# Hybrid short-convolution and SSD step: pools, early loads and the order of splits where the projection hands over to the mixing

## The chip, the cores and the metric

The kernel runs on one core of a Trainium2 chip. The core has TensorE (PE in the profile, with its weight loads as PEld), VectorE (DVE), ScalarE (ACT), GpSimd (POOL) and SyncE (SP, which here issues all DMAs), each with an instruction stream of its own, in order; semaphores tie the streams together. The metric is the time of one execution in device microseconds, the median of several runs.

## The reference

One layer over 2048 prompt tokens and 64 sample tokens, width 1024, all float32. Cut to what matters:

```python
h = rmsnorm(x, norm_in_w) * (1 + scale) + shift        # shift, scale, gate = split(c @ w_mod + b_mod)
proj = h @ w_in                                         # (1024, 7184): the large product
b_gate, c_gate, h_a, g_a, z, xbc_raw, dt_raw = split(proj)
y_a = rmsnorm(b_gate * dwconv3(c_gate * h_a) * silu(g_a), norm_a_w)
xs, bs, cs = split(silu(dwconv4(xbc_raw) + conv_b_b))
y = ssd(xs, softplus(dt_raw + dt_bias), -exp(a_log), bs, cs) + d_skip * xs   # causal scan in chunks
y_b = rmsnorm(y * silu(z), norm_b_w)
x = x + gate * (concat(y_a, y_b) @ w_out)               # (2048, 1024): the output product
y_out = rmsnorm(x, norm_f_w)
```

`c` has one row for the prompt and one for the sample. The states of both convolutions and of the scan are outputs too.

## The kernel before, in words

Every large product is made of three: each operand is split into a high part (rounded by ACT's copy) and a low part (the rest, by DVE), and high x high, high x low and low x high are added up in PSUM. The weights of the output product are split the same way by `split_wo(k, raw)`: ACT writes the high part `woh` (line 1274), DVE the low part `wol` (line 1275), from a raw row block of 512 KB that SP has loaded (`wo_raw`). There are 16 such blocks.

**Projection (`phase_project`).** The tokens go through in two passes. A pass visits 28 pairs of feature tiles (`work[g]`, 56 in all): z, x/B/C and the four parts of the convolution branch. The features and tokens of a pair are cut in quarters so that seven products (`s` = 0 to 6) do the work of eight; sums and differences of quarters (A22, A12, A11, S1 to S4) are kept in SBUF. In each slot `s` the code issues a product on PE (line 282), prepares a weight quarter of the next pair (`w_hi` on ACT, line 248; `w_lo` on DVE, line 239), runs hooks, runs work from a queue with an estimated cost (`run_bg`), and empties PSUM (`evac`: copies `keep` on ACT at line 307, adds on DVE at line 315). `w_load(g + 2)` loads the raw weights of a pair, 1 MB, two pairs ahead. Everything is written in program order; no scheduler moves it.

The rows that are worked on live in tiles `row0` to `row7`. Hooks in pairs 51 to 53 compute the gate (`gate_load`, `gate_part`): eight blocks of `w_mod` are multiplied with `c`, then four adds put the bias on, tile `gb` (line 635); each bias piece is loaded just ahead of its add (line 633) and the result stored right after it (line 636).

**The last pair (`last_pair`, g = 55).** It is done as eight plain products from S1, A22, A12 and A11 in that order (line 1169), each emptied from its own two PSUM banks: `evac_last(1, ...)` after S1 and A22, `evac_last(0, ...)` after the others (lines 487 and 489, into the rows `c_row`, which are then stored to `va_d`, line 492). Its weights come from `last_w` (lines 175 and 176). While PE works, nine of the 16 output weight blocks are split, and the decays of the first chunk, tiles `lt`, are computed by `decay_first` (lines 1195 and 1197: eight Relu and one Exp each).

**Mixing (`phase_mix`).** For each chunk of 128 tokens and each half of the heads: `ssd1` (PE heads and transposes, lines 1335 to 1339; DVE then makes `bc`, `xd`, `lt`, `xe`, lines 1344 to 1351), `ssd2` (PE, lines 1363 to 1369), `join1` and `join2` on DVE; and for each token tile the output product with both branches, `out_mm` (lines 1438 and 1445; `vah` is the split convolution branch, `vbh` the split SSD branch). `ra` is the inverse norm of a branch (`inv_rms`: PE, DVE, POOL). It starts with the 64 sample tokens, mixed with the first chunk; there the other seven weight blocks are split. `vb_s` is the sample's SSD branch, loaded from `vb_d` and split by ACT and DVE (lines 1411 and 1415).

Pools are stacked from both sides of SBUF. A tile of a later pool waits for the readers of the tiles it overlies; a tile with the same tag waits for the readers of the one before it.

Of the kernel before, what the change touches and what calls it, by code (L numbers as in the profile page):

```python
# [27 lines left out]
def kernel(  # L28
# [76 lines left out]
    def phase_project():  # L105
# [14 lines left out]
        lp = pool(stack, "lp", bufs=1, reuse_waits="tile")  # L120
        hs1 = pool(hstack, "hs1", bufs=1, side="right", reuse_waits="tile")
# [60 lines left out]
        for i in (0, 1, 6, 7, 2, 3, 4, 5):  # L182
            row(i, [128, 1094], f"row{i}_")
        pad(lp, "pad_l", 128)
        raws = [hs1.tile([128, KT, 256], F32, tag=f"raw{i}", name=f"raw{i}") for i in range(2)]
        pad(hs1, "pad_h", 96)
# [317 lines left out]
        def dt_parts():  # L504
# [6 lines left out]
            def load():  # L511
# [386 lines left out]

        sample = sample_parts()
# [19 lines left out]
        def mod_half(half, pieces):  # L919
# [11 lines left out]
            m = stats.tile([128, 2, 4, 2], F32, tag="mcol", name="mcol", bufs=1)  # L931
# [225 lines left out]

        def last_pair():
# [3 lines left out]
            pss = {fh: [bank(no + u) for u in range(2)] for fh, no in (((0, 1), 4), ((1, 1), 2), ((0, 0), 0), ((1, 0), 6))}  # L1162
# [10 lines left out]
            p1 = mix["sp1"] = pool(ctx, "sp1", side="right", reuse_waits="tile")  # L1173
            state = mix["state"] = p1.tile([128, 2, 512], F32, tag="state", name="state")
            fast = [p1.tile([128, 8, 128], F32, tag="lt", name="lt", bufs=2) for _ in range(2)]
            p1.tile([128, 8, 128], F32, tag="rb", name="rb_")
            xbs = [p1.tile([128, 8, 128], F32, tag="xb", name="xb", bufs=2) for _ in range(2)]
            pad(p1, "pad_p", 224)
# [11 lines left out]
            def load_decay(hf):  # L1190
                SP.dma_start(out=fast[hf], in_=r_d[hf * 8:hf * 8 + 8, :].partition_broadcast(128))

            def decay_first(hf):
                for h in range(8):
                    ACT.activation(out=fast[hf][:, h, :], in_=fast[hf][:, h, :], func=AF.Relu, scale=-1.0,
                                   bias=acum[:, 0, 8 * hf + h:8 * hf + h + 1])
                ACT.activation(out=fast[hf], in_=fast[hf], func=AF.Exp, scale=-1.0)
                held[0, hf] = fast[hf]

            va = mix["va"] = state[:, 1, :].rearrange("p (s t) -> p s t", t=NS_TOK)  # L1200
# [476 lines left out]
```

## Time and profile before

| what | value |
|---|---|
| median of 3 runs | 1759.02 us (1757.54 to 1760.46) |
| the profiled execution, whole | 1758.51 us |
| its span, first to last instruction | 1756.7 us |
| TensorE's mean granted clock | 0.994 of full |
| DVE busy | 74% of the span |
| ACT busy | 47% |
| DMA, mean over the span | 125 GB/s |
| HBM read, written | 164.31 MB, 54.15 MB |

The span is what the profiler saw of the instructions; the time is taken around the whole execution and is 1.8 us longer. "A <- B" in the waits reads: A stood idle until B had finished. Rows of a timeline give the start, the duration, the engine, the line, output <- inputs, and in brackets the idle time ahead and what ended it. Times in them count from the start of the span.

### The profile page before, as it was taken

The page shows a single profiled execution, that of the slowest core. Times are in us where ns is not written, and L with a number is a line of the kernel's source. Part 1 is how long each engine was busy: PE and PEld are TensorE (multiplying, and loading weights), DVE is VectorE, ACT ScalarE, POOL GpSimd, SP SyncE. Part 2 cuts the span into 40 slices and gives each one's busy share as a digit, 9 for nine tenths or more (in the row PEclk, how much of TensorE's full clock was granted, in tenths as well). Part 3 has the DMA queues.
Part 4 walks back from the last instruction along what each step waited for, and adds up shares of the span by engine and source line. Part 5 has one row for each costly group of instructions (what it writes and reads, how often), then busy time and mean ns, then how long its engine had stood idle before and what let it go on. Part 6 is the DMA issues. An engine that isn't in the chain of part 4 may idle for free.

```text
span 1756.7 us, 27034 instructions
## 1 busy us (share of the span) xinstructions
PE 1713.1 (98%) x10585; PEld 1511.0 (86%) x10585; DVE 1307.6 (74%) x2026; ACT 828.4 (47%) x1579; POOL 102.9 (6%) x224
## 2 busy tenths in 40 slices
PE   5999999999999999999999999999899999999998
PEld 4788888887888899999999999989588888888887
DVE  5787779776677746687768767646788888888885
ACT  5644344444653645334333444325455555545552
POOL 0000000000000000010001000000011111101011
PEclk9999999999999999999999999999899999999999
DMA  9223323233538832312322242424653343434341
GB/s 340 73 73 96 96 82 99 84 104 102 168 127 296 294 100 80 97 54 95 100 75 74 74 121 79 131 73 161 200 192 125 139 150 126 161 107 169 110 150 36
DMA packets 186867, 220.21 MB, mean 125 GB/s; under 512 B 21316, under 2 KB 152372, under 8 KB 186740
## 3 DMA queue, kind: packets, MB, share of 16 engines
q1 hardware_dynamic: 186740, 218.49, 37.7%
q8 instruction: 83, 1.36, 0.3%
q14 instruction: 44, 0.36, 0.1%
HBM read 164.31 MB, written 54.15 MB: 124 GB/s over the span
## 4 chain that ended last, share of the span: by engine, by line
PE 89%; DVE 3%; ACT 3%; DMA 2%; issue 2%; SPq 0%; POOL 0%; POOLq 0%; ACTq 0%; DVEq 0%
PE bank L282 58%; PE mm L1438 14%; PE mm L1445 7%; PE sd L1363 2%; PE sd L1367 2%; PE sd L1369 2%; DMA praw<-in_w_mod_dram 1%; PE sd L1335 1%; PE sd L1339 1%; PE bank L1048 1%; PE bank L535 0%; PE bank L536 0%; DVE loS L1035 0%; PE bank L826 0%; PE sd L1337 0%
## 5 line engine op out<-in xcount | busy, mean ns | idle before, releaser
L282 PE MATMUL bank<-hiS,w 128*128 128x272 f32 (+1 forms) x2560 | 596.6, 322 | 5.7 <-ACT keep L307 5.6
L282 PEld LDWEIGHTS bank<-hiS,w 128*128 128x128 f32 x2560 | 431.0, 189 | 41.5 <-ACT keep L307 8.2
L282 PE MATMUL bank<-hiA,w 128*128 128x272 f32 (+1 forms) x1920 | 447.8, 321 | 3.1 <-DVE z_row L315 2.7
L282 PE MATMUL bank<-loS,w 128*128 128x272 f32 (+1 forms) x1280 | 411.4, 321 | 0.0
L282 PEld LDWEIGHTS bank<-hiA,w 128*128 128x128 f32 x1920 | 322.8, 188 | 30.8 <-DVE z_row L315 3.2
L239 DVE TENSOR_TENSOR w<-raw,w 128x512 fp32r<-128x512 f32 x318 | 217.7, 687 | 161.7 <-ACT w L248 150.8
L248 ACT CAST w<-raw 128x512 fp32r<-128x512 f32 x318 | 196.3, 622 | 240.2 <-PE bank L282 134.3
L282 PE MATMUL bank<-loA,w 128*128 128x272 f32 (+1 forms) x960 | 308.1, 321 | 0.0
L282 PEld LDWEIGHTS bank<-loS,w 128*128 128x128 f32 x1280 | 241.4, 189 | 16.1
L282 PEld LDWEIGHTS bank<-loA,w 128*128 128x128 f32 x960 | 180.5, 188 | 12.2
L307 ACT COPY keep<-bank 128x272 f32<-128x272 f32 (+1 forms) x240 | 106.0, 451 | 133.4 <-PE bank L282 132.8
L388 DVE SCALAR_TENSOR_TENSOR acc<-raw_row,par,acc 128x1024 f32<-128x1024 f32 (+1 forms) x96 | 126.4, 1317 | 2.0
L239 DVE TENSOR_TENSOR raw<-raw 128x512 f32<-128x512 f32 x161 | 111.0, 689 | 3.7
L1438 PE MATMUL mm<-woh,vah 128*128 128x512 f32 (+1 forms) x272 | 109.5, 403 | 0.0
L1438 PE MATMUL mm<-wol,vah 128*128 128x512 f32 (+1 forms) x272 | 106.5, 392 | 0.0
L1438 PE MATMUL mm<-woh,vbh 128*128 128x512 f32 (+1 forms) x256 | 103.7, 405 | 0.0
L1438 PE MATMUL mm<-wol,vbh 128*128 128x512 f32 (+1 forms) x256 | 100.5, 392 | 0.0
L1297 ACT ACTIVATE lt<-rb,acum 128x128 f32<-128x128 f32 x240 | 73.3, 388 | 3.7 <-DMA rb<-r_d 3.2
L248 ACT CAST w<-t 128x512 fp32r<-128x512 f32 x53 | 32.8, 618 | 76.2 <-PE bank L282 76.2
L1445 PE MATMUL mm<-woh,vah 128*128 128x512 f32 (+1 forms) x272 | 67.3, 390 | 0.0
L1445 PE MATMUL mm<-woh,vbh 128*128 128x512 f32 (+1 forms) x256 | 63.3, 389 | 0.0
L1445 PEld LDWEIGHTS mm<-woh,vah 128*128 128x128 f32 (+1 forms) x272 | 50.2, 185 | 11.5
(298 smaller groups left out, 2375.2 us busy)
## 6 DMA issues: line engine op xcount, KB each, us to landing
raw<-in_w_in_dram SPq DMA_DIRECT2D x56, 1024.0 KB
xb_d<-acc SPq DMA_DIRECT2D x32, 512.0 KB
xb<-xb_d SPq DMA_DIRECT2D x32, 512.0 KB
rb<-r_d SPq DMA_DIRECT2D x30, 512.0 KB
xt<-in_x_prompt_dram SPq DMA_DIRECT2D x16, 512.0 KB
praw<-in_w_mod_dram SPq DMA_DIRECT2D x16, 512.0 KB
z_d<-z_row SPq DMA_DIRECT2D x16, 512.0 KB
va_d<-c_row SPq DMA_DIRECT2D x16, 512.0 KB
```

The source lines that it names most:

```text
L239: DVE.tensor_tensor(out=out, in0=a, in1=b, op=ALU.subtract)
L248: ACT.copy(out=w[:, 0], in_=w_src(g, j))
L282: PE.matmul(ps[:, 0:n], w[:, a, k, :], h[:, k, o:o + n], start=(s in (0, 1, 5) and k == 0 and i == 0), stop=(k == 3 and i == 2), skip_grou ...
L307: ACT.copy(out=keep[s][:, o:o + n], in_=b["y" if s == 1 else "x"][:, 0:n])
L388: DVE.scalar_tensor_tensor(out=acc[:, 0:n], in0=r[:, k:k + n], scalar=cb_w(k, t), in1=acc[:, 0:n], op0=ALU.mult, op1=ALU.add)
L1048: PE.matmul(ps, w[:, a, k, :], x, start=(i == 0 and k == 0 and n == 0), stop=(i == 1 and k == 3 and n == 2))
L1297: ACT.activation(out=lt[:, h, :], in_=rb[:, h, :], func=AF.Relu, scale=-1.0, bias=acum[:, c, h0 + h:h0 + h + 1])
L1363: PE.matmul(py4[64 * e:64 * e + 64, j, :], xd[:, 2 * j + e, :], lt[:, 2 * j + e, :], start=True, stop=True)
L1367: PE.matmul(po4[:, j, :], state[:, hf, j * 128:(j + 1) * 128], xb[:, 6 + j // 2, :], start=True, stop=True)
L1369: PE.matmul(ps[:, g * 256:(g + 1) * 256], bc[:, g, :], xe[:, 4 * g:4 * g + 4, :].rearrange("p h q -> p (h q)"), start=True, stop=True)
L1438: PE.matmul(ps[:n], hl[:, 0, k, 0:n], wo[k0 + k][i][:, nn * 512:(nn + 1) * 512], start=(k == 0 and i == 0), stop=False)
L1445: PE.matmul(ps[:n], hl[:, 1, k, 0:n], wo[k0 + k][0][:, nn * 512:(nn + 1) * 512], start=False, stop=(k == 7))
```

## The change

Three things are changed, all around the end of the projection.

1. *Pools.* Rows 2 to 5 and the raw weights go into a pool `top` that stays open to the end, where the last pair and the mixing use the same tiles again (`row4` for `rb` and weight blocks, `row5` for `state`, `raw0` and `raw1` for `xb` and `lt`, rows 2 and 3 for output weight 6). The pool `sp1` goes. The raw weights of a pair become two tiles of 512 KB with a DMA each. Some small tiles move from `stats` to `lp`. In PSUM the last pair takes its banks in another order, and the mixing phase opens its tag `mm` first.
2. *Loads.* The four bias pieces of the gate are loaded with the gate's first block. In pair 54 SP loads the first half of chunk 0 (`load_first(0)`) and the first four output weight blocks (`early_o`), and ACT computes the first decay in slot 4 of that pair. In the mixing phase three weight blocks are loaded ahead of `vb_s`.
3. *Splits.* Eleven blocks are split in the last pair (0 to 10), 11 to 13 ahead of the sample's `ra`, and 14 and 15 after the first half of chunk 0. In a slot, `last_w` comes after `evac`.

```diff
         def row(i, shape, name, dtype=F32):
             flush(i)
-            return (hs1 if 2 <= i <= 5 else lp).tile(shape, dtype, tag=f"row{i}", name=name)
+            return (top if 2 <= i <= 5 else lp).tile(shape, dtype, tag=f"row{i}", name=name)
...
-            raw = raws[g % 2] = hs1.tile([128, KT, 256], F32, tag=f"raw{g % 2}", name="raw")
+            raw = raw_pair()
             col = work[g][0]
-            SP.dma_start(out=raw, in_=w_in[:, col:col + 256].rearrange("(k p) f -> p k f", p=128))
+            for i in range(2):
+                SP.dma_start(out=raw[i], in_=w_in[512 * i:512 * i + 512, col:col + 256].rearrange("(k p) f -> p k f", p=128))
...
         def gate_load(k, r):
+            if k == 0:
+                gb = gate_held["gb"] = row(4, [128, 256], "gb")
+                for j in range(4):
+                    SP.dma_start(out=gb[32 * j:32 * j + 2, 0:256], in_=b_mod[:, 2 * D + j * 256:2 * D + (j + 1) * 256]
+                                 .partition_broadcast(2).rearrange("p o n -> p (o n)"))
...
-                gb = row(4, [128, 256], "gb")
+                gb = gate_held["gb"]
                 for j in range(4):
                     q, col = slice(32 * j, 32 * j + 2), slice(j * 256, (j + 1) * 256)
-                    SP.dma_start(out=gb[q, 0:256], in_=b_mod[:, 2 * D + j * 256:2 * D + (j + 1) * 256]
-                                 .partition_broadcast(2).rearrange("p o n -> p (o n)"))
                     DVE.tensor_tensor(out=gb[q, 0:256], in0=ps[q, 0:256], in1=gb[q, 0:256], op=ALU.add)
                     SP.dma_start(out=g_d[:, col], in_=gb[q, 0:256])
...
+        hook_at(54 * 7, lambda: load_first(0))
+        for k in range(4):
+            hook_at(54 * 7 + 1 + k // 2, lambda k=k: early_o(k))
...
+        def load_first(hf):
+            fast[hf] = top.tile([128, 8, 128], F32, tag="raw1", name="lt", bufs=2)
+            SP.dma_start(out=fast[hf], in_=r_d[hf * 8:hf * 8 + 8, :].partition_broadcast(128))
+            xbs[hf] = top.tile([128, 8, 128], F32, tag="raw0", name="xb", bufs=2)
+            SP.dma_start(out=xbs[hf], in_=xb_d[0, :, hf])
+            loads[0, hf] = [xbs[hf], None]
...
+        def early_o(k):
+            raw_o[k] = row(2 + k, [128, D], "wo_raw")
+            SP.dma_start(out=raw_o[k], in_=w_out[k * 128:(k + 1) * 128, :])
...
-            pss = {fh: [bank(no + u) for u in range(2)] for fh, no in (((0, 1), 4), ((1, 1), 2), ((0, 0), 0), ((1, 0), 6))}
+            pss = {fh: [bank(no) for no in nos] for fh, nos in (((0, 1), (4, 5)), ((1, 1), (6, 7)), ((0, 0), (3, 2)), ((1, 0), (0, 1)))}
...
-            homes = ["w6", "rb", "row6", "row7", "w6", "rb", "row6", "row7", "w6"]
+            homes = [None] * 4 + ["w6", "row7", "row6", "row4", "w6", "row7", "row6", "row4"]
...
-            for k in range(9):
+            load_o(4)
+            load_o(5)
+            load_first(1)
+            load_o(6)
+            for k in range(11):
                 split_wo(k, raw_o.pop(k))
-                if k + 4 < 9:
+                if k == 2:
+                    load_o(7)
+                elif k == 3:
...
+                elif 4 <= k <= 7:
                     load_o(k + 4)
-                if k < 2:
-                    decay_first(k)
-                elif k == 5:
+                if k == 5:
+                    decay_first(1)
                     evac_last(1, True)
                     evac_last(1, False)
-            evac_last(0, False)
+                elif k == 9:
+                    evac_last(0, False)
...
-                elif s > 0:
+                evac(p, g, s)
+                if tg >= last and s > 0:
                     last_w(s - 1)
-                evac(p, g, s)
+                if (g, s) == (last - 1, 4):
+                    decay_first(0)
...
+        for k, tag, bufs in ((12, "xr", 2), (13, "xr", 2), (14, "gate", 1)):
+            load_o(k, tag, bufs)
         vb = sp.tile([128, 8, 128], F32, tag="vb", name="vb_s")
         SP.dma_start(out=vb[:, :, 0:n], in_=vb_d)
         for hf in range(2):
             prefetch_z(0, hf)
...
+        load_o(15, "nf", 1)
...
         va = prefetch_va(0)
+        for k in (11, 12, 13):
+            split_wo(k, raw_o[k])
         ra = inv_rms(sqa, n, "ra")
         t0 = take_a(16, pa, ra)
-        for k, nxt, tag, bufs in ((9, 13, "xr", 2), (10, 14, "xr", 2), (11, 15, "gate", 1), (12, None, "", 0)):
-            split_wo(k, raw_o[k])
...
-            split_wo(k, raw_o[k])
-            if nxt:
-                load_o(nxt, tag, bufs)
...
-        for k in (13, 14, 15):
+        for k in (14, 15):
             split_wo(k, raw_o[k])
```

How the instructions stand, before and after, at three places. Line numbers of the changed kernel are its own.

SP's queue from the gate's last two bias pieces (`gb` the bias tile, `g_d` the gate in DRAM) into the last pair, before:

```order
L633 DMA gb<-in_b_mod_dram 2x256
L636 DMA g_d<-gb 2x256
L1188 DMA wo_raw<-in_w_out_dram 128x1024
L1191 DMA lt<-r_d 128x1024
L1188 DMA wo_raw<-in_w_out_dram 128x1024
L1191 DMA lt<-r_d 128x1024
L1188 DMA wo_raw<-in_w_out_dram 128x1024 x2
L1215 DMA xb<-xb_d 128x1024 x2
```

and after, from the four stores of the gate:

```order
L654 DMA g_d<-gb 2x256 x4
L1183 DMA lt<-r_d 128x1024
L1185 DMA xb<-xb_d 128x1024
L1197 DMA wo_raw<-in_w_out_dram 128x1024 x4
L1222 DMA wo_raw<-in_w_out_dram 128x1024 x2
L1183 DMA lt<-r_d 128x1024
L1185 DMA xb<-xb_d 128x1024
```

The bias loads no longer stand between the stores, and the first decay's rows, the first `xb` and four weight blocks are issued in the pair before the last.

ACT from the fourth weight of the last pair (line 175, in the changed kernel 178) to the first output weight blocks (`woh`), before:

```order
L175 CAST w_11394<-raw 128x512
L462 ACTIVATE g_row<-g_row 128x1090
L175 CAST w_11429<-raw 128x512
L175 CAST w_11459<-raw 128x512
```

and, a few rows on,

```order
L462 ACTIVATE g_row<-g_row 128x1090
L1274 ACTIVATE woh_11683<-wo_raw,par 128x1024
L1195 ACTIVATE lt<-lt,acum 128x128 x8
L1197 ACT_TABLE_LOAD
L1197 ACTIVATE lt<-lt 128x1024
L1274 ACTIVATE woh_11685<-wo_raw,par 128x1024
L1195 ACTIVATE lt<-lt,acum 128x128 x8
L1197 ACTIVATE lt<-lt 128x1024
```

After, from the same weight:

```order
L178 CAST w_11535<-raw 128x512
L1190 ACTIVATE lt<-lt,acum 128x128 x8
L1192 ACT_TABLE_LOAD
L1192 ACTIVATE lt<-lt 128x1024
L477 ACT_TABLE_LOAD
L477 ACTIVATE g_row<-g_row 128x1090
L178 CAST w_11578<-raw 128x512
```

The first decay stands ahead of the Silu of `g_row` and of the last two weights, with a table load on either side of it.

DVE from the split of the sample's SSD branch to the first chunk's second half, before:

```order
L1415 TENSOR_TENSOR vbh<-vb_s,vbh 128x8x64
L100 TENSOR_SCALAR ms<-sd 64x1
L1275 SCALAR_TENSOR_TENSOR wol_11700<-wo_raw,par,woh_11699 128x1024
L1275 SCALAR_TENSOR_TENSOR wol_11702<-wo_raw,par,woh_11701 128x1024
L1275 SCALAR_TENSOR_TENSOR wol_11704<-wo_raw,par,woh_11703 128x1024
L1275 SCALAR_TENSOR_TENSOR wol_11706<-wo_raw,par,woh_11705 128x1024
L1378 SCALAR_TENSOR_TENSOR yt<-xb,dcol,sd 128x128 x4
L1344 TENSOR_TENSOR bc<-sd,cst 128x256
L1346 TENSOR_TENSOR xd<-sd,dt_t 128x512
L1349 TENSOR_TENSOR lt<-lt,bc 128x512 x2
```

and after:

```order
L1444 TENSOR_TENSOR vbh<-vb_s,vbh 128x8x64
L1302 SCALAR_TENSOR_TENSOR wol_11841<-wo_raw,par,woh_11840 128x1024
L1302 SCALAR_TENSOR_TENSOR wol_11843<-wo_raw,par,woh_11842 128x1024
L1302 SCALAR_TENSOR_TENSOR wol_11845<-wo_raw,par,woh_11844 128x1024
L102 TENSOR_SCALAR ms<-sd 64x1
L1407 SCALAR_TENSOR_TENSOR yt<-xb,dcol,sd 128x128 x4
L1373 TENSOR_TENSOR bc<-sd,cst 128x256
L1375 TENSOR_TENSOR xd<-sd,dt_t 128x512
L1378 TENSOR_TENSOR lt<-lt,bc 128x512 x2
```

Three splits instead of four, and they stand ahead of `ms`, the DVE step of `ra`, where four stood behind it.

More of the change, by code (lines that the diff above doesn't have):

```diff
@@ L81, in pad @@
         p.tile([128, n // 4], F32, tag=name, name=name, bufs=1)
+    pad(const, "pad_c", 64)
     def ca_w(k, t):
@@ L181, in phase_project, with raw_pair @@
             h_tile(q, 544)
[L182 to L186, printed above, removed]
+        for i in (0, 1, 6, 7, 2, 3, 5, 4):
+            row(i, [128, 1152 if i in (2, 3) else 1094], f"row{i}_")
+        for _ in range(2):
+            lp.tile([128, 4, 2], F32, tag="ss", name="ss", bufs=2)
+            lp.tile([128, 4], F32, tag="ms4", name="ms4", bufs=2)
+        lp.tile([128, 2, 4, 2], F32, tag="mcol", name="mcol")
+        lp.tile([128, NH], F32, tag="dtb", name="dtb")
+        lp.tile([128, NH], F32, tag="alog", name="alog")
+        pad(lp, "pad_l", 64)
+        pad(top, "pad_t", 192)
+        def raw_pair():
+            return [top.tile([128, 4, 256], F32, tag=f"raw{i}", name="raw", bufs=2) for i in range(2)]
+        for _ in range(2):
+            raw_pair()
+        pad(top, "pad_e", 224)
         def load_rows(chunks, rows):
@@ L1156, in last_w, with decay_first @@
             split(src, w[:, 0], w[:, 1])
+        raw_o, fast, xbs = {}, {}, {}
+        def load_first(hf):
[4 more added lines that the diff above has]
+            loads[0, hf] = [xbs[hf], None]
+        def decay_first(hf):
+            for h in range(8):
+                ACT.activation(out=fast[hf][:, h, :], in_=fast[hf][:, h, :], func=AF.Relu, scale=-1.0,
+                               bias=acum[:, 0, 8 * hf + h:8 * hf + h + 1])
+            ACT.activation(out=fast[hf], in_=fast[hf], func=AF.Exp, scale=-1.0)
+            held[0, hf] = fast[hf]
+        def early_o(k):
+            raw_o[k] = row(2 + k, [128, D], "wo_raw")
+            SP.dma_start(out=raw_o[k], in_=w_out[k * 128:(k + 1) * 128, :])
         def last_pair():
             w, units = wstate[last]["w"], PASS[1][2]
-            pss = {fh: [bank(no + u) for u in range(2)] for fh, no in (((0, 1), 4), ((1, 1), 2), ((0, 0), 0), ((1, 0), 6))}
+            pss = {fh: [bank(no) for no in nos] for fh, nos in (((0, 1), (4, 5)), ((1, 1), (6, 7)), ((0, 0), (3, 2)), ((1, 0), (0, 1)))}
             for q, h, js in (("S1", 1, (0, 1)), ("A22", 1, (4, 5)), ("A12", 0, (2, 3)), ("A11", 0, (0, 1))):
@@ L1172, in last_pair @@
             hstack.close()
[L1173 to L1178, printed above, removed]
             wop = pool(ctx, "wop", side="right", reuse_waits="tile")
-            for k in (0, 1, 2, 3, 4, 5, 7, 8, 9, 10, 11, 12, 13, 14, 15, 6):
+            for k in (0, 1, 2, 3, 4, 5, 7, 8, 9, 10, 11, 12, 13, 14, 15):
                 wo[k] = (wop.tile([128, D], F32R, tag=f"woh{k}", name=f"woh{k}"),
                          wop.tile([128, D], F32R, tag=f"wol{k}", name=f"wol{k}"))
-            raw_o = {}
-            homes = ["w6", "rb", "row6", "row7", "w6", "rb", "row6", "row7", "w6"]
+            homes = [None] * 4 + ["w6", "row7", "row6", "row4", "w6", "row7", "row6", "row4"]
             def load_o(k):
-                raw_o[k] = (p1 if homes[k] == "rb" else lp).tile([128, D], F32, tag=homes[k], name="wo_raw")
+                raw_o[k] = (top if homes[k] == "row4" else lp).tile([128, D], F32, tag=homes[k], name="wo_raw")
                 SP.dma_start(out=raw_o[k], in_=w_out[k * 128:(k + 1) * 128, :])
[L1190 to L1200, printed above, removed]
             ends = [as_[3][3][1]["last"](f) for f in range(2)]
@@ L1514, in phase_mix @@
             prefetch_z(0, hf)
-        raw_o = {}
-        def load_o(k, tag, bufs):
-            raw_o[k] = sp.tile([128, D], F32, tag=tag, name="wo_raw", bufs=bufs)
-            SP.dma_start(out=raw_o[k], in_=w_out[k * 128:(k + 1) * 128, :])
-        for k, tag, bufs in ((9, "xr", 2), (10, "xr", 2), (11, "gate", 1), (12, "nf", 1)):
-            load_o(k, tag, bufs)
+        load_o(15, "nf", 1)
         vah = split_act(va, n, "vah")
```

43 lines of the change are left out of this document (22 added, 21 removed).

## The prediction, on record before the run

> **What bounds the kernel now.** I read the page first (busy shares and the chain), then what TensorE (PE) waited for, then each engine in order of time around PE's long pauses.
>
> ```profile
> span 1756.7 us, 27034 instructions
> PE 1713.1 (98%) x10585; PEld 1511.0 (86%) x10585; DVE 1307.6 (74%) x2026; ACT 828.4 (47%) x1579; POOL 102.9 (6%) x224
> ...
> PE 89%; DVE 3%; ACT 3%; DMA 2%; issue 2%; SPq 0%; POOL 0%; POOLq 0%; ACTq 0%; DVEq 0%
> ```
>
> PE is busy for 98% and the chain runs through it for 89%, and the change takes no matmul away. So it can win only where PE stands still. The waits of PE (total, times, longest, in us):
>
> ```profile
> PE bank L220 <- DVE xt L215: 14.7, 8, 13.0
> PE bank L282 <- ACT keep L307: 5.6, 4, 4.1
> PE sd L1335 <- DVE c_row L489: 3.5, 1, 3.5
> PE sd L1363 <- DVE lt L1349: 3.3, 1, 3.3
> ```
>
> The first is the start, where x must arrive. The other three long ones lie within 70 us of each other, where the projection ends and the mixing begins; call them pauses 1, 2 and 3. Each is followed by a slow clock (stretches; PE's busy time and matmuls, ..., granted clock, DMA share, GB/s):
>
> ```profile
> 1188.90:1192.15 3.25, 3.23 (x14) 3.24 (x15) 3.18 (x6) 1.91 (x6) 0.32 (x2) 0.51 0.02 5
> 1196.00:1199.25 3.25, 3.25 (x28) 3.25 (x28) 1.58 (x3) 0.62 (x1) 0.00 (x0) 1.00 0.00 0
> ...
> 1229.60:1233.10 3.50, 0.07 (x1) 0.00 (x0) 2.89 (x4) 2.03 (x3) 0.00 (x0) 0.99 0.01 2
> 1233.10:1236.90 3.80, 3.71 (x15) 3.12 (x16) 3.27 (x8) 0.91 (x2) 0.00 (x0) 0.56 0.73 221
> ...
> 1254.00:1260.30 6.30, 6.29 (x26) 4.33 (x27) 6.30 (x9) 3.29 (x4) 0.00 (x0) 0.50 0.74 245
> ```
>
> After pause 1, 14 matmuls took the 3.25 us in which 28 run later: 1.6 us lost on top of the pause.
>
> **Pause 1: the gate's bias (loads moved ahead).** DVE, ACT and PE around it:
>
> ```profile
> 1178.66 0.41 DVE L635 TENSOR_TENSOR gb<-bank,gb 2x256 f32<-2x256 f32 x1 [1.98 <-PE bank L627]
> 1180.70 0.42 DVE L635 TENSOR_TENSOR gb<-bank,gb 2x256 f32<-2x256 f32 x1 [1.63 <-DMA gb<-in_b_mod_dram]
> ...
> 1185.19 1.35 DVE L439 SCALAR_TENSOR_TENSOR c_row<-u_row,par,c_row 128x1090 f32<-128x1090 f32 x1
> ...
> 1187.96 0.62 ACT L248 CAST w<-raw 128x512 fp32r<-128x512 f32 x1 [9.43 <-DVE raw L239]
> 1188.48 0.67 ACT L307 COPY keep<-bank 128x272 f32<-128x272 f32 x2
> ...
> 1184.52 0.29 PE L282 MATMUL bank<-hiS,w 128*128 128x272 f32 x1
> 1188.91 0.60 PE L282 MATMUL bank<-hiS,w 128*128 128x272 f32 x1 [4.11 <-ACT keep L307]
> ```
>
> Each of the four adds waits for its own little load, which SP issues only after the store of the one before. With all four loads issued two pairs earlier, the adds follow one another: 1178.66 + 4 x 0.41 = 1180.3, and all that DVE has queued behind (L439 at 1185.19) comes 4.9 us sooner. ACT's cast then starts at 1183.1 and the two copies end at 1184.3; PE wants them at 1184.65. Pause and slow clock go, 4.1 + 1.6 = 5.7 us. The margin is 0.4 us, so the bounds are 5.7 and 4.7 (the two copies a further 1.4 us late, as one L439 more on DVE would make them). I take 5.7, since every duration is a row's. From here all times are 5.7 earlier.
>
> **What pays for pause 2.** The first chunk's decay moves into the pair before the last:
>
> ```profile
> 1211.38 2.45 ACT L1195 ACTIVATE lt<-lt,acum 128x128 f32<-128x128 f32 x8 [0.71 <-DMA lt<-r_d]
> 1213.85 1.28 ACT L1197 ACT_TABLE_LOAD   x1
> 1215.14 1.06 ACT L1197 ACTIVATE lt<-lt 128x1024 f32<-128x1024 f32 x1
> ...
> 1226.76 1.16 ACT L1274 ACTIVATE woh<-wo_raw,par 128x1024 fp32r<-128x1024 f32 x1 [1.92 <-DMA wo_raw<-in_w_out_dram]
> ...
> 1217.27 1.28 DVE L1275 SCALAR_TENSOR_TENSOR wol<-wo_raw,par,woh 128x1024 fp32r<-128x1024 f32 x1 [5.29 <-ACT woh L1274]
> 1232.70 1.48 DVE L489 TENSOR_TENSOR c_row<-bank,c_row 128x272 f32<-128x272 f32 x4
> ...
> 1229.38 0.29 PE L1169 MATMUL bank<-hiA,w 128*128 128x272 f32 x1
> 1233.19 1.22 PE L1335 MATMUL sd<-xb 128*128 128x128 f32 x4 [3.52 <-DVE c_row L489]
> 1241.55 1.10 PE L1363 MATMUL sd<-lt,xd 128*64 128x128 f32 x16
> ...
> 1243.84 0.71 PE L1335 MATMUL sd<-xb 128*128 128x128 f32 x4
> 1248.73 2.00 PE L1445 MATMUL mm<-woh,vah 128*64 128x512 f32 x8
> ```
>
> and from the chain of waits, in order of time:
>
> ```profile
> 1225.46 4.84 DMA wo_raw<-in_w_out_dram
> ...
> 1264.64 3.67 PE mm L1438 x16
> ```
>
> Pause 2 comes because DVE reads the last bank only at 1232.7: its nine splits waited for ACT's halves, and those for loads and for two decays. It costs 3.5 us, and the same stretch (heads, then one output product) takes 8.4 us (1233.19 to 1241.55) where it later takes 6.8 (1243.84 to 1250.6): 1.6 more, 5.1 in all.
>
> After: ACT does decay 0 four slots before the last pair: 2.45 + 1.28 + 1.06 = 4.8 us, and one more table load of 1.28 to return to Silu. Its cover is an ACT that worked 0.62 of 3.25 us there (second stretch above). Silu then ends near 1199.5 instead of 1195.7; the weight splits for the last pair's second product end near 1203.6 and 1205.6, and PE, starting that pair at 1199.7, wants them at 1205.7 and 1208.7. If the cover failed, PE would wait up to 2 us.
>
> Splits 0 to 3 find their loads landed. ACT starts at 1206; DVE does six splits at 1.2 to 1.3 from 1207.3 to 1214.6 and reads half of the banks (1.5 as in the L489 row, and the sample's share). ACT meanwhile does decay 1 (4.8) and delivers split 6 at 1218.3; DVE's splits 6 to 9 end near 1223.2, and it reads the banks of the first feature tile by 1223.9, the others by 1224.6, since PE only ends at 1223.8. Now another wait is latest: split 10, whose load goes out after split 6 (1219.5) and by the slowest load here (4.84 us in the chain) lands at 1224.4. ACT's cast of the sample's va stands behind it, which PE needs at 1225. I leave 0.3 us of pause; bounds 0 and 1.5. Gain 4.8 (3.6 to 5.1). The banks are renumbered, but PE's first head waits for the first of the last four reads in both: before, it began 0.5 us after the first of them did (1232.70, 1233.19).
>
> **Pause 3: two splits fewer, but other loads in front.**
>
> ```profile
> 1233.51 1.07 SPq L492 DMA_DIRECT2D va_d<-c_row  x2
> 1236.45 0.58 SPq L1512 DMA_DIRECT2D vb_s<-vb_d  x1
> ...
> 1239.57 0.62 ACT L1411 CAST vbh<-vb_s 128x512 fp32r<-128x512 f32 x1 [3.79 <-DMA vb_s<-vb_d]
> 1244.76 0.68 ACT L1455 ACTIVATE t<-mm,ra 64x512 f32<-64x512 f32 x1 [4.58 <-POOL ra L101]
> 1245.35 4.26 ACT L1274 ACTIVATE woh<-wo_raw,par 128x1024 fp32r<-128x1024 f32 x4
> ...
> 1254.01 1.97 PE L1363 MATMUL sd<-lt,xd 128*64 128x128 f32 x16 [3.28 <-DVE lt L1349]
> 1257.43 0.99 PE L1438 MATMUL mm<-woh,vbh 128*64 128x512 f32 x1
> 1262.64 2.01 PE L1445 MATMUL mm<-woh,vbh 128*64 128x512 f32 x8
> ```
>
> It costs 3.3 us, then 1.2 (1254.01 to 1257.43, 3.4 us, against 2.3 from 1241.55 to 1243.84) and 1.5 for 16 matmuls in 5.2 us (to 1262.64) against 3.67 in the chain: 6.0. Before, DVE reached lt after four splits (4.3 us on ACT) that ACT held back for ra. Now three splits stand ahead of ra, which wins 1.2 us, but ACT has its cast of vb_s ahead of those three, and SP has three loads of 512 KB ahead of vb_s. The first waits for the store of the rows it overlies, as vb_s did (2.9 us, 1233.51 to 1236.45). So: stores at 1224.0 and 1224.7, loads at 1226.9, 1227.7 and 1228.1, vb_s at 1228.6. It took 3.1 us (1236.45 to 1239.57) with no load ahead; with three ahead I estimate 4.9, from the 4.8 above: 1233.5 (bounds 3.1 and 6.2: 1231.7 and 1234.8). Behind it: cast 0.7, ACT's first half 1.1, DVE's three splits 3.7, and ra, its POOL step, ACT's two copies and DVE to the end of lt about 4.2: 1243.2. PE, unhindered, is there at 1223.8 + 0.3 + 6.8 + 2.3 + 6.8 = 1240.0. Pause 3 stays, 3.2 us (1.4 to 4.5), with its slow clock: no gain (bounds: 4.6 gained, if it is 1.4 and the clock stays; 1.2 lost).
>
> A rule bears on that clock. The Trainium skill (TensorE: Matmul & The Clock Gate, Part 1) says that the clock halves after an idle window of some 3.4 us, which runs free of the program, so that a somewhat shorter stop may spare it. By it the 2.7 us behind pause 3 could be saved too, and the time would be 1745.8; this trace has 0.50 after a stop of 3.28, against the letter of it.
>
> **The rest, at nothing.** The 56 weight loads go out in two halves: 56 more issues of some 0.4 us on an SP that mostly waits, for tiles loaded two pairs ahead; 0, bounds 0.5 either way. Tiles that change pools add no instruction. Splits 9 and 10 come into the last pair (2 x 1.22 on DVE), in idle like the 5.29 above. Splits 14 and 15 stay behind the first mixing products, end near 1247.5 by the same durations and are wanted from 1248.3 on. PE's 1.8 us around the span (time 1758.51, span 1756.7) remain.
>
> **Sum.** 5.7 + 4.8 + 0 = 10.5 us. From the profiled 1758.51: 1748.0; the median of the runs is 0.5 higher, 1759.02, so 1748.5.
>
> **Rivals.**
> - *Pause 3 shrinks too* (vb_s lands as fast as before): 1.4 us with no slow clock, 4.6 more: 1743.9; gone altogether 1742.5. For it: DMA stood idle in pause 2 (share 0.01). Against it: the loads put ahead.
> - *One pause comes back in another place*: ACT's early decay and its extra table load make the last pair's weights or the last bank reads late, and PE stops for 3 to 5 us in the last pair: 1752 to 1754. For it: margins of 2 us or less. Against it: ACT's idle time.
> - *Slower*: the halved weight loads come late in every pair. From 0.2 us in each of some 54 pairs (10.8 us) the gain is eaten; at 0.3 (16.2 us) it is 1764.7. Against it: PE's waits show no weight load in the loop.
> - *Nothing gained* (the change does not do what it says): the adds still wait, for the gate's product or another load, and splits 9 and 10 are late: 1757 to 1760.
>
> **Chances.** Forecast (1746 to 1751) 0.52; pause 3 shrinks 0.25; one comes back 0.14; nothing 0.05; slower 0.04. The range 1742 to 1754 holds the first three but for their edges. A measurement of this kernel tells 0.2%, 3.5 us, from no change: faster 0.91, same 0.05, slower 0.04.
>
> **What would show it.** After: no 4 us wait of PE on keep, the four gb adds within 2 us; no wait of 3 us on c_row; a wait on lt of about 3 us with clock 0.5 behind it, and ACT waiting for vb_s before three woh. Wrong would be a new wait of PE inside the last pair (weights w) or in the weight loop (raw).

## The result, and the profile after

| | median | range | ratio to before (95% interval) |
|---|---|---|---|
| before | 1759.09 us | 1757.54 to 1760.46 | |
| changed | 1747.25 us | 1745.23 to 1747.72 | 0.9933 [0.9919, 0.9946] |

The forecast was 1748.5 us. (One disturbed execution of the changed kernel, of 3451 us, is left out; the median is that of the other three.) The profiled execution of the changed kernel took 1747.72 us with a span of 1746.0, 10.7 us less than the span before. First the page, then TensorE's waits (engine and line, what it waited for: total, times, longest in us):

```profile
span 1746.0 us, 27150 instructions
...
PE 89%; DVE 5%; ACT 3%; issue 2%; DMA 2%; POOL 0%; SPq 0%; POOLq 0%; ACTq 0%; DVEq 0%
```

```profile
PE bank L234 <- DVE xt L229: 15.2, 8, 13.6
PE sd L1392 <- DVE lt L1378: 5.0, 2, 4.7
...
PE bank L297 <- ACT keep L322: 1.5, 3, 0.9
```

The waits of 4.1 us on `keep` and 3.5 us on `c_row` are gone; the wait on `lt` is there, and longer: 4.7 us where it was 3.3. Where the time came from is read by setting the same instruction of both traces side by side:

| PE begins | before | after | ahead by |
|---|---|---|---|
| the last pair | 1205.45 | 1199.68 | 5.8 |
| the first heads | 1233.19 | 1223.73 | 9.5 |
| `ssd2` of the first half | 1241.55 | 1230.46 | 11.1 |
| `ssd2` of the second half | 1254.01 | 1244.36 | 9.7 |
| the last group of the first SSD output product | 1262.64 | 1251.49 | 11.15 |
| `ssd2` of chunk 1's second half | 1286.70 | 1275.86 | 10.8 |

Three of these rows as the changed kernel's trace has them:

```profile
1230.46 1.09 PE L1392 MATMUL sd<-lt,xd 128*64 128x128 f32 x16
...
1251.49 2.00 PE L1474 MATMUL mm<-woh,vbh 128*64 128x512 f32 x8
...
1275.86 1.17 PE L1392 MATMUL sd<-lt,xd 128*64 128x128 f32 x16 [0.26 <-DVE lt L1378]
```

So pause 1 paid 5.8 us, pause 2 and its slow clock 5.3, pause 3 nothing on balance (it lost 1.4 and got 1.5 back in the clock), and 0.3 was lost later: 0.26 us of the `lt` total above stands just ahead of that last row.

Pause 1, in the timeline (start, duration, engine and line):

```profile
1178.66 1.77 DVE L653 TENSOR_TENSOR gb<-bank,gb 2x256 f32<-2x256 f32 x4 [1.98 <-PE bank L647]
...
1183.23 0.62 ACT L263 CAST w<-raw 128x512 fp32r<-128x512 f32 x1 [4.70 <-DVE raw L254]
1183.76 1.47 ACT L322 COPY keep<-bank 128x272 f32<-128x272 f32 x4
```

The four adds run in a row, and ACT's cast starts at 1183.23 (it was 1187.96).

The last pair: ACT, DVE, and PE's change to the heads.

```profile
1191.72 2.45 ACT L1190 ACTIVATE lt<-lt,acum 128x128 f32<-128x128 f32 x8 [0.18 <-DMA lt<-r_d]
...
1205.20 6.34 ACT L1301 ACTIVATE woh<-wo_raw,par 128x1024 fp32r<-128x1024 f32 x6
...
1222.17 1.15 ACT L1301 ACTIVATE woh<-wo_raw,par 128x1024 fp32r<-128x1024 f32 x1 [1.75 <-DMA wo_raw<-in_w_out_dram]
...
1204.31 0.69 DVE L179 TENSOR_TENSOR w<-raw,w 128x512 fp32r<-128x512 f32 x1 [0.69 <-ACT w L178]
...
1222.12 1.13 DVE L504 TENSOR_TENSOR c_row<-bank,c_row 128x272 f32<-128x272 f32 x3
1223.93 0.44 DVE L504 TENSOR_TENSOR c_row<-bank,c_row 128x272 f32<-128x272 f32 x1 [0.68 <-PE bank L1210]
...
1223.73 0.60 PE L1364 MATMUL sd<-xb 128*128 128x128 f32 x4
```

ACT makes six high parts without waiting for a load. DVE has read three of the four last banks before PE is done, and now DVE waits for PE (0.68) where PE waited for DVE.

Pause 3: SP's loads, then ACT, DVE, PE.

```profile
1225.88 2.69 SPq L1544 DMA_DIRECT2D wo_raw<-in_w_out_dram  x3
1228.62 0.57 SPq L1549 DMA_DIRECT2D vb_s<-vb_d  x1
...
1235.61 0.62 ACT L1440 CAST vbh<-vb_s 128x512 fp32r<-128x512 f32 x1 [8.78 <-DMA vb_s<-vb_d]
1236.14 3.23 ACT L1301 ACTIVATE woh<-wo_raw,par 128x1024 fp32r<-128x1024 f32 x3
...
1243.63 1.28 DVE L1378 TENSOR_TENSOR lt<-lt,bc 128x512 f32<-128x512 f32 x2
...
1239.24 0.40 PE L1474 MATMUL mm<-woh,vah 128*64 128x512 f32 x1
1244.36 1.98 PE L1392 MATMUL sd<-lt,xd 128*64 128x128 f32 x16 [4.72 <-DVE lt L1378]
```

ACT stands still for 8.78 us for `vb_s`, which left SP at 1228.62 behind three blocks; only then come the three splits, `ra` and `lt`.

### The profile page after: what moved, and what is told of

It reads as the page before. It is cut to its first block, busy times and chain, and to the rows that moved or that the text cites. A ratio compares the mean times of both kernels' runs of the same rounds, so it can differ in the third digit from the quotient of the medians.

```text
span 1746.0 us, 27150 instructions
## 1 busy us (share of the span) xinstructions
PE 1708.2 (98%) x10585; PEld 1507.9 (86%) x10585; DVE 1307.9 (75%) x2026; ACT 830.8 (48%) x1581; POOL 102.6 (6%) x224
## 4 chain that ended last, share of the span: by engine, by line
PE 89%; DVE 5%; ACT 3%; issue 2%; DMA 2%; POOL 0%; SPq 0%; POOLq 0%; ACTq 0%; DVEq 0%
PE bank L297 57%; PE mm L1467 13%; PE mm L1474 6%; PE sd L1392 2%; PE sd L1396 2%; PE sd L1398 2%; PE bank L1210 1%; PE sd L1364 1%; PE sd L1368 1%; PE bank L1069 1%; DMA raw<-in_w_in_dram 1%; DVE w L254 0%; PE bank L550 0%; PE bank L551 0%; DVE loS L1056 0%
## 5 line engine op out<-in xcount | busy, mean ns | idle before, releaser
L1467 PE MATMUL mm<-woh,vah 128*128 128x512 f32 (+1 forms) x238 | 95.9, 403 | 0.0
L1467 PE MATMUL mm<-wol,vah 128*128 128x512 f32 (+1 forms) x238 | 93.0, 391 | 0.0
L1474 PE MATMUL mm<-woh,vah 128*128 128x512 f32 (+1 forms) x238 | 65.2, 390 | 0.0
L1492 ACT ACTIVATE t<-xr 128x512 f32<-128x512 f32 (+1 forms) x32 | 20.3, 633 | 81.7 <-DVE xr L1491 81.7
```

The costliest lines, as they stand in the source:

```text
L1467: PE.matmul(ps[:n], hl[:, 0, k, 0:n], wo[k0 + k][i][:, nn * 512:(nn + 1) * 512], start=(k == 0 and i == 0), stop=False)
L1474: PE.matmul(ps[:n], hl[:, 1, k, 0:n], wo[k0 + k][0][:, nn * 512:(nn + 1) * 512], start=False, stop=(k == 7))
L1492: ACT.activation(out=t[:n], in_=xr[:n, s], func=AF.Square, accum_out=ss[:n, nn:nn + 1])
```

## Experiments

Theories. For pause 1: the adds' loads. For pause 2: A1, ACT's early decay pays for it, or A2, the early loads of the weight blocks. For pause 3: Q, `vb_s` is late because of its place in SP's queue; B, the DMA engines are full there and the order changes nothing; C, the wait would only move to the splits.

### Pause 1 alone

The kernel before with the early bias loads and nothing else:

```diff
+            if k == 0:
+                gb = gate_held["gb"] = row(4, [128, 256], "gb")
+                for j in range(4):
+                    SP.dma_start(out=gb[32 * j:32 * j + 2, 0:256], in_=b_mod[...])
...
-                    SP.dma_start(out=gb[q, 0:256], in_=b_mod[...])
```

> The kernel before with one part of the change alone: the four bias pieces of the gate are loaded with the gate's first block. Theory (pause 1 is the four adds that wait for their loads): the 4.1 us wait of PE on keep goes, with the slow clock behind it; the last pair starts near 1199.7 us instead of 1205.45, pauses 2 and 3 stay as they were, and the time falls by 5.7 us, from 1759.0 to 1753.3. Rival (the pause only moves: what DVE and ACT win is given back at the next wait): 1757 to 1759.

Measured: 1753.89 us, before 1758.60 in the same runs; ratio 0.9975 [0.9965, 0.9984]. 4.7 us where 5.7 was expected; the interval reaches from 2.8 to 6.2 us. The rival falls. PE's waits:

```profile
PE sd L1338 <- DVE c_row L489: 3.9, 1, 3.9
PE sd L1366 <- DVE lt L1352: 3.5, 2, 3.3
```

Pause 1 is gone. In this trace PE was 0.56 us late from the start of the kernel on (the same matmul ahead of pause 1 began at 1179.39 before and at 1179.95 here) and began the last pair at 1200.24, 5.21 us ahead, so that pause 1 paid the same 5.8 us as in the changed kernel. Pause 2 is 0.4 us longer than before (3.9 for 3.5), and the clock after it was slow for 6.8 us, twice as long as in the profile of before, while behind pause 3 it was slow for half as long (last section): 1.3 us lost and 1.2 won back. In this profile the missing 1.0 us is thus the late start and 0.3 us in chunk 1, not pause 1.

### Pause 2: the decay or the loads

The changed kernel with the first decay back in the last pair:

```diff
-                if (g, s) == (last - 1, 4):
-                    decay_first(0)
...
+                if k == 0:
+                    decay_first(0)
                 if k == 5:
                     decay_first(1)
```

> The changed kernel with the first chunk's decay put back into the last pair (behind split 0), its loads staying early. Theory A (pause 2 is paid for by ACT's early decay): ACT's decay of 3.5 us and a table load of 1.3 then stand ahead of splits 1 to 10, DVE reaches the last four reads of banks near 1226 us instead of 1222.1, and PE, done at 1223.7, waits 2.3 to 2.7 us for c_row; with one slow stretch of 3.4 us (1.7 lost) or none: 1750 to 1752 against 1747.5. Rival B (the early loads and the new order of splits did it, ACT has room): 1747 to 1748 and no wait on c_row.

Measured: 1747.98 us (before 1758.42), ratio 0.9937 [0.9924, 0.9951]; the changed kernel in the same runs 1747.32, 0.9936 [0.9924, 0.9949]. No difference, and no wait of PE on `c_row`: with the loads early, the early decay is not needed, and A1 falls. This execution began 2.0 us late (PE was in the last pair at 1201.7), so 2.0 is to be taken off:

```profile
1196.47 1.12 ACT L477 ACTIVATE g_row<-g_row 128x1090 f32<-128x1090 f32 x1 [2.93 <-DVE g_row L330]
...
1203.85 1.14 ACT L1301 ACTIVATE woh<-wo_raw,par 128x1024 fp32r<-128x1024 f32 x1
1204.89 2.43 ACT L1190 ACTIVATE lt<-lt,acum 128x128 f32<-128x128 f32 x8
...
1209.60 5.30 ACT L1301 ACTIVATE woh<-wo_raw,par 128x1024 fp32r<-128x1024 f32 x5
```

ACT begins its first split at 1201.85 on the other's time scale, 3.35 us ahead of the changed kernel, because no decay and no second table load delays the Silu and what follows it. Doing the decay early costs ACT as much ahead of the splits as it saves between them.

The loads of blocks 0 to 3 put back into the last pair, the decay staying early:

```diff
-        for k in range(4):
-            hook_at(54 * 7 + 1 + k // 2, lambda k=k: early_o(k))
...
             load_first(1)
+            for k in range(4):
+                early_o(k)
             load_o(6)
```

> The changed kernel with the loads of the first four output weight blocks put back into the last pair, behind its first two and the second decay's rows. Theory A (pause 2 comes from splits that wait for loads): they go out from 1206 us on and land at 1209.5 to 1214, DVE's split 0 starts 4 us later than at 1206.5, all that follows it is 4 to 5 us late, less what DVE and ACT stood idle between 1215 and 1222, and PE waits 2.5 to 4.6 us for c_row, with one slow stretch: 1751.5 to 1754. Rival B (ACT and DVE catch up in their idle time): under 1 us of wait, 1747.5 to 1748.5.

Measured: 1753.17 us, ratio 0.9970 [0.9959, 0.9982]: 5.9 us slower than the changed kernel. Without the early loads the pause is back, as A2 says. PE's waits, ACT's first split and DVE's last reads:

```profile
PE sd L1364 <- DVE c_row L504: 5.6, 1, 5.6
PE sd L1392 <- DVE lt L1378: 2.9, 1, 2.9
```

```profile
1211.49 1.16 ACT L1301 ACTIVATE woh<-wo_raw,par 128x1024 fp32r<-128x1024 f32 x1 [6.30 <-DMA wo_raw<-in_w_out_dram]
...
1229.18 1.48 DVE L504 TENSOR_TENSOR c_row<-bank,c_row 128x272 f32<-128x272 f32 x4
```

With the decay early but the loads late ACT waits 6.3 us for block 0 and pause 2 is back, larger than before. (In this run the four loads stand behind four others, blocks 4 and 5, `lt` and `xb`, where before the change block 0 was the first load of the last pair; so the run shows that the early loads are needed, but not what they alone are worth. What the new order of the splits and of the bank reads adds was not run by itself. Pause 3 is shorter here by 1.8, which is why the time rises less than pause 2 and its clock.)

### Pause 3: the order of the loads, or of the work

First, `vb_s` ahead of the three blocks in SP's queue (tiles stay):

```diff
+            raw_o[k] = sp.tile([128, D], F32, tag=tag, name="wo_raw", bufs=bufs)
         vb = sp.tile([128, 8, 128], F32, tag="vb", name="vb_s")
         SP.dma_start(out=vb[:, :, 0:n], in_=vb_d)
+        for k, tag, bufs in outs:
+            SP.dma_start(out=raw_o[k], in_=w_out[k * 128:(k + 1) * 128, :])
```

> The changed kernel, with the load of vb_s issued ahead of the loads of blocks 12 to 14 instead of behind them; tiles and all else stay. Theory A (vb_s is late because of its place in the queue, and ACT and DVE stand still behind it): vb_s lands by 1229 to 1231 us instead of 1235.6, ACT then waits only for the landing of blocks 12 and 13, which I put at 1232 to 1234, lt is ready near 1239.6 and the 4.7 us wait of PE on lt shrinks to 0 to 1.5 us: 1741.8 to 1743.5 against 1747.5. Rival B (the DMA engines are full there, 0.92 to 0.94 of their time, and all four transfers end together near 1235 whatever their order): block 13 is then what is late, the wait stays at 3.5 to 5 us, and the time at 1746 to 1748.

Measured: 1741.64 us (1741.18 to 1742.64; before 1758.60), ratio 0.9905 [0.9892, 0.9919]. Q holds, and this beats both kernels: 5.7 us faster than the changed one (by the medians; the changed one's 1747.32 was taken beside a before of 1758.42). ACT, DVE, PE:

```profile
1230.33 0.62 ACT L1440 CAST vbh<-vb_s 128x512 fp32r<-128x512 f32 x1 [2.92 <-DMA vb_s<-vb_d]
...
1238.34 1.28 DVE L1378 TENSOR_TENSOR lt<-lt,bc 128x512 f32<-128x512 f32 x2
...
1240.15 1.09 PE L1392 MATMUL sd<-lt,xd 128*64 128x128 f32 x16
```

`vb_s` lands 4.2 us after its issue at 1226.17, `lt` is ready 0.5 us ahead of PE, and PE does not stop.

Second, the loads as in the change, but the split of `vb_s` behind `ra`:

```diff
-        vbh = split_act(vb, n, "vbh")
-        split_dve(vb, n, vbh)
         ssd2(0, 0)
...
         t0 = take_a(16, pa, ra)
+        vbh = split_act(vb, n, "vbh")
+        split_dve(vb, n, vbh)
```

> The changed kernel, with the split of vb_s (ACT's cast and DVE's low part) moved from ahead of splits 11 to 13 to behind the step that uses ra; the loads keep their order. Theory A (pause 3 is the wait for vb_s ahead of the splits): splits 11 to 13 now start when their own blocks land, 13 near 1233.5, and lt, which still has the split of vb_s in front, is ready near 1241: the wait shrinks from 4.7 to about 1.5 us with no slow clock, 1743.4 (1742.5 to 1745). Rival B (the loads end together near 1235): 4 to 5 us of wait and 1747 to 1748.5.

Measured: 1742.72 us, ratio 0.9911 [0.9897, 0.9924]; the wait on `lt` there is 0.25 us. ACT shows when the blocks came:

```profile
1229.89 1.15 ACT L1301 ACTIVATE woh<-wo_raw,par 128x1024 fp32r<-128x1024 f32 x1 [1.64 <-DMA wo_raw<-in_w_out_dram]
1232.55 1.15 ACT L1301 ACTIVATE woh<-wo_raw,par 128x1024 fp32r<-128x1024 f32 x1 [1.50 <-DMA wo_raw<-in_w_out_dram]
```

Blocks 12 and 13 land at 1229.9 and 1232.5, one after the other: here what was issued first arrived first, and B falls.

Third, `ra`, join 1 and `lt` ahead of the split of `vb_s` and of splits 12 to 15:

```diff
-        for k in (11, 12, 13):
-            split_wo(k, raw_o[k])
+        split_wo(11, raw_o[11])
         ra = inv_rms(sqa, n, "ra")
         t0 = take_a(16, pa, ra)
         join1(0, 0)
         ssd1(0, 1)
+        vbh = split_act(vb, n, "vbh")
+        split_dve(vb, n, vbh)
         join2(0, 0)
         prefetch(1, 0)
-        for k in (14, 15):
+        for k in (12, 13, 14, 15):
```

> The changed kernel with the order of the work between the first half of chunk 0 and its second half changed: split 11, ra and what uses it, join 1, the second half's heads and lt, only then the split of vb_s, join 2 and splits 12 to 15. No load moves. Theory A (lt is late only because ra stands behind vb_s and three splits): lt is ready near 1237 us, 2.6 us ahead of PE, pause 3 and its slow clock are gone and the splits are still in time (the last, 15, near 1244.2, wanted at 1245): 1741.8 (1741 to 1743). Rival C (the pause only moves on, to PE's wait for the low parts wol 12 to 15 in the first output product of the SSD branch): a wait of 1 to 4 us there, 1743 to 1747.

Measured: 1742.64 us, ratio 0.9911 [0.9896, 0.9927]. `lt` is ready at 1236.8 and the four splits end at 1244.0; PE waits for neither. C falls. Only the later wait on `lt`, 0.4 us in chunk 1, is left.

Both cures at once, the queue of the first and the order of the third:

> Both cures of pause 3 at once: vb_s loaded ahead of blocks 12 to 14, and ra, join 1 and lt ahead of the split of vb_s and of splits 12 to 15. If nothing but pause 3 is left there to win, it is as fast as the one with vb_s loaded first (1741.6): 1741 to 1742. If that one was still held by something within the chunk, it is up to 1 us faster; if DVE's late splits now make PE wait, up to 1 us slower.

Measured: 1742.32 us (before 1758.42), ratio 0.9906 [0.9893, 0.9920], no different from the first alone. The two cures do not add up, since the first alone leaves PE no wait there; this profile has 1.0 us of the later wait on `lt`.

The changed kernel once more, beside these:

> The changed kernel once more, beside the three below: 1747.5 us. If the slow clock after pause 3 lasts one stretch of 3.4 us in some executions and two in others (the trace before showed 3.4, 3.4 and 6.8), its times spread over some 2 us, while the kernel without pause 3 (vb_s loaded first, 1741.2 to 1742.6) spreads less.

Measured: 1747.32 us, 1746.48 to 1748.69, so 2.2 us wide against 1.5 without pause 3. The direction fits, but four or five times each are few.

### What a stop costs: the slow clock

The kernel with `vb_s` first, with 2, 3 and 4 needless repeats of one split's low part on DVE ahead of `ra` (the same values are written). The grid that theory W speaks of is shown in the last section.

```diff
+        for _ in range(2):   # 3, 4
+            DVE.scalar_tensor_tensor(out=wo[13][1], in0=raw_o[13], scalar=nb_w(5), in1=wo[13][0].bitcast(F32),
+                                     op0=ALU.mult, op1=ALU.subtract)
         ra = inv_rms(sqa, n, "ra")
```

> The kernel with vb_s loaded first (1741.6 us; PE never stops there, lt is ready 0.5 us before PE comes), with the low part of split 13 written two times more ahead of ra: 2.4 us more work on DVE, the same values. PE should stop 1.9 us for lt. Theory W (the clock is set at the edges of a grid of 3.41 us that runs free of the program, and halves after a stretch in which PE was busy less than some 40%): a stop of 1.9 us leaves every stretch over 44% busy, so no slow clock, and the time is 1743.5. Rival S (a stop of any length is followed by a slow stretch): 1745.2.

> As the run before with three times more: 3.6 us on DVE, a stop of 3.1 us. Theory W: whether a stretch of the grid is under 40% busy depends on where the stop falls in it, in some 7 of 10 executions it is, and a slow stretch of 3.4 us costs 1.7: 1744.7 in some executions, 1746.4 in others, median near 1746, with a wider spread than the kernel without a stop. Rival T (the stop must itself be longer than 3.4 us): never slow, 1744.7 with a spread like that of the kernel without a stop.

> As the runs before with four times more: 4.9 us on DVE, a stop of 4.3 us, about pause 3's own length in the changed kernel. Theory W and rival T: always one slow stretch of 3.4 us or two, 1.7 to 3.4 lost beside the stop: 1747.6 to 1749.3. If a stop costs its length alone: 1745.9.

| repeats | stop in the profile | clock at half, in the profile | median (range) | ratio to before |
|---|---|---|---|---|
| 0 | none | never | 1741.64 (1741.18 to 1742.64) | 0.9905 [0.9892, 0.9919] |
| 2 | 1.54 us | never | 1744.24 (1743.86 to 1746.04) | 0.9922 [0.9909, 0.9934] |
| 3 | 3.66 us | 3.4 us | 1747.09 (1745.56 to 1747.92) | 0.9932 [0.9918, 0.9945] |
| 4 | 4.71 us | 6.8 us | 1747.79 (1747.15 to 1748.29) | 0.9939 [0.9926, 0.9951] |

The row without repeats is from another set of runs (before 1758.60; the others beside 1758.66). Rival S falls by the profile of the first, a stop of 1.54 us with no slow clock behind it (PE's stop, then the 3.41 us of that trace in which PE was busy least):

```profile
1241.92 1.26 PE L1392 MATMUL sd<-lt,xd 128*64 128x128 f32 x16 [1.54 <-DVE lt L1378]
```

```profile
1239.81:1243.22 3.41, 1.83 (x20) 0.95 (x18) 2.97 (x6) 3.41 (x6) 0.00 (x0) 1.00 0.73 273
```

That a stop of 4.7 costs more than itself is shown by the last (6.15 us over no stop). The medians of the first two are 0.7 and 1.1 us above W's, though the first stop came out shorter than expected (1.54 for 1.9 us); whether some of their executions fell into a slow stretch is not seen, as each kernel has one profile. Rival T is not tested by the second, whose stop came out at 3.66; it falls by stops of 2.87, 3.27 and 3.28 us in other traces, each with slow clock behind it (pause 3 with the weights loaded late, with the early bias loads alone, and before).

What the slow stretches cost beside the stop is read from the start of `ssd2` of the second half to the last group of the first SSD output product, the same matmuls in each trace: 5.69 us with no slow stretch (`vb_s` first, 1240.15 to 1245.84), 7.13 (changed kernel) and 7.53 (3 repeats) with one, 8.23 (4 repeats) and 8.63 (before) with two. So one cost 1.4 to 1.8 us and two cost 2.5 to 2.9.

## Why the prediction was right, and where it was not

- *Pause 1* (5.7 forecast): 5.8, by the mechanism named. ACT's cast was due at 1183.1 and came at 1183.23. Right.
- *What pays for pause 2*: the early decay did delay the last pair's weights as told (the last low part ready at 1205.0, forecast 1205.6, wanted 1208.7), and ACT's idle time covered it. But that it pays was wrong: put back, the time stayed; the loads of four blocks a pair ahead are what paid, and without them pause 2 returned. (How much of it they pay without the new order of splits and bank reads is open.) The prediction credited both together. It let ACT start the splits late, at 1206, but never compared that with the decay left in place: moved ahead of ACT's Silu and weights, it takes 3.35 us from the start of the splits, about what it saved between them.
- *Pause 2* (4.8 forecast, 3.6 to 5.1): 5.3, above the upper bound by 0.2. The term mis-sized is split 10's load, forecast to land at 1224.4 after 4.84 us; it went out at 1218.64 and was there at 1222.17, 3.5 us. The 0.3 us of pause left for it did not come. The other 0.2 is PE's first heads, which begin 0.12 us after the last matmul of the pair began (1223.61, 1223.73), not after it ended.
- *Pause 3* (3.2 us forecast, 1.4 to 4.5; gain 0): 4.7 us, outside the bounds; the gain came out at 0.1 because two errors cancelled. The place in the queue was right (`vb_s` issued at 1228.62, forecast 1228.6), and PE came at 1239.6, forecast 1240.0. Mis-sized was the transfer: 6.97 us where 4.9 was taken with 6.2 as the limit. The 4.84 of a single load was stretched to stand for the last of four. What came behind `vb_s` was sized too long, 9.7 us where it took 8.75 (1235.61 to 1244.36), which hid part of the error. The four are 3 x 0.524 + 0.262 = 1.84 MB, and the stretches behind their issue ran at (us; busy us and counts of PE, its weight loads, DVE, ACT and POOL; clock, DMA share, GB/s)

```profile
1223.70:1230.40 6.70, 6.70 (x36) 4.22 (x34) 5.97 (x9) 1.62 (x3) 0.00 (x0) 1.00 0.92 268
1230.40:1232.80 2.40, 2.40 (x24) 1.77 (x23) 0.00 (x0) 0.00 (x0) 0.00 (x0) 1.00 0.94 335
```

  so 1.84 MB takes 5.5 to 6.9 us, and that happens to fit the 6.97 counted from `vb_s`'s own issue; counted from the first block's issue (1225.88) `vb_s` took 9.7 us. The sum leaves out the two row stores ahead of the four. By the packets of this trace the stores' 1.03 MB move until 1227.2, then the blocks at 275 GB/s; the small packets of `vb_s` (1024 of 256 bytes, where a block has 4096-byte ones) are hardly among them before 1232, and it lands at 1235.61. The 3.1 us of before was no bare transfer either: there too the stores still moved for the first 1.1 us of it. So the price needs all that is ahead in the queue, stores too. The other error is the clock: one slow stretch of 3.4 us behind this pause, where 6.3 us of it followed before and was forecast again. It gave back 1.5 us.
- *The rest at nothing*: PE is at 1177.76 in both traces with the same matmul, so the halved weight loads cost nothing. The 0.3 us lost in chunk 1 was not forecast.
- *Rivals.* Pause 3 did not shrink, no pause appeared in the last pair or in the weight loop, and the slower case and the one with nothing gained did not come.
- *The rule weighed* (1745.8 if the clock stays full behind pause 3): the clock did halve, after a stop of 4.7 us. With the grid of the last section one could have said beforehand that the second slow stretch behind pause 3 depends on where in the grid the pause falls, so that counting on it again was not safe.

The sum was right (10.5 forecast, 10.7 in the spans, 11.8 in the medians). Its terms for pauses 1 and 2 were right in cause and nearly in size, except that the early decay pays nothing; pause 3's nothing was right by luck.

## What to carry to other kernels

A load whose consumer holds up a whole engine in order goes ahead of larger loads that are wanted later; to price its place in a queue, add up all the bytes ahead of it, stores too, at the rate of the same stretch, and do not take the time of one load. Work moved to an earlier idle stretch gains nothing if it delays, on its own engine, the work that it was to make room for: here the moved decay gained nothing, and pause 2 went only with the moved loads. A stop of PE costs its length; the stops of 2.87 us and more here were also followed by one or two slow stretches, at 1.4 to 2.9 us, and the one of 1.54 was not, so that the last microsecond of a pause may be worth more than the first.

## What the runs showed of the hardware

The granted clock changes on a grid. Followed in steps of 0.2 us, every slow stretch behind a pause, in eight profiles, lasted 3.41 or 6.83 us, whatever the pause; in the trace before they began at 1188.66 and 1233.03, 44.37 us apart, 13 x 3.413. Before each change stands one stretch of that grid. Here from the trace before (all three pauses), from the changed kernel, from the one with the weights loaded late, and from the ones with 3 and 4 repeats (columns as above; the last number but two is the clock in that stretch):

```profile
1185.25:1188.66 3.41, 0.00 (x0) 0.00 (x0) 3.38 (x4) 0.70 (x2) 0.00 (x0) 1.00 0.00 1
1188.66:1192.07 3.41, 3.15 (x14) 3.16 (x15) 3.34 (x6) 2.10 (x6) 0.32 (x2) 0.50 0.02 5
...
1250.10:1253.51 3.41, 0.63 (x3) 0.13 (x1) 3.41 (x9) 1.18 (x2) 0.00 (x0) 1.00 0.98 376
1253.51:1256.92 3.41, 2.91 (x18) 2.41 (x19) 3.41 (x6) 3.16 (x4) 0.00 (x0) 0.50 0.85 304
1256.92:1260.34 3.42, 3.42 (x9) 1.92 (x8) 3.42 (x5) 0.61 (x1) 0.00 (x0) 0.50 0.63 176
```

```profile
1240.63:1244.04 3.41, 0.00 (x0) 0.00 (x0) 2.81 (x9) 2.32 (x4) 0.55 (x1) 1.00 0.28 79
1244.04:1247.46 3.42, 3.10 (x19) 2.59 (x20) 3.42 (x6) 2.21 (x3) 0.00 (x0) 0.50 0.57 228
```

```profile
1222.79:1226.20 3.41, 1.28 (x11) 1.05 (x9) 1.80 (x2) 3.41 (x4) 0.00 (x0) 1.00 0.29 109
```

```profile
1241.43:1244.84 3.41, 1.23 (x16) 0.83 (x16) 2.91 (x6) 3.41 (x6) 0.00 (x0) 1.00 0.72 269
```

```profile
1239.47:1242.88 3.41, 0.09 (x1) 0.00 (x0) 2.78 (x8) 1.25 (x3) 0.54 (x1) 1.00 0.00 0
1242.88:1246.29 3.41, 2.02 (x17) 1.69 (x17) 3.41 (x7) 3.28 (x4) 0.00 (x0) 0.50 0.80 306
1246.29:1249.70 3.41, 3.41 (x8) 2.19 (x9) 3.41 (x6) 0.00 (x0) 0.00 (x0) 0.50 0.51 156
```

The clock halved after stretches in which PE was busy for 0 to 1.28 us of 3.41 (up to 38%), and it came back after stretches with 3.10 us or more (91%); after 2.91 (85%) and 2.02 (59%) it stayed at half for one more. The stop of 1.54 us left no stretch of that length under 1.83 us busy (54%), and the clock stayed. So a stop of 3.28 us (pause 3 before, with 0.63 us busy in its stretch) halved the clock, and how many slow stretches followed depended on where in the grid PE started again: in the profile before one each behind pauses 1 and 2 and two behind pause 3, with the early bias loads alone two behind pause 2 and one behind pause 3.

The Trainium skill (TensorE: Matmul & The Clock Gate, Part 1) gives a free-running window of 3413 ns, which these traces agree with to the hundredth. It lets the clock fall after an idle window; here it fell after windows with up to 1.28 us of work, so the measurement decides: the window need not be empty. Where between 38% and 54% busy the limit lies was not tried with a stop. The first 40 us of the kernel draw no sharp line either: in the changed kernel a stretch with 1.46 us busy (32.31 to 35.72) halved the clock, but in the run with `ra` first one with 1.45 (29.23 to 32.64) left it and the next, with 1.99 (58%), halved it. So the busy time of the profile is not all that the clock goes by.
